# A decoder layer on one core: the retention's gates and values as seven-product pairs, another bank order in a pair's plain steps, six raw weight tiles, later first sums

## The chip, the cores and the metric

The kernel runs on one core of a Trainium2 chip. The time is device microseconds of one execution of the whole program; lower is better. All data are float32. TensorE (PE in the profile) runs the matmuls, VectorE (DVE) and ScalarE (ACT) the elementwise work, GpSimd (POOL) a few small operations and the DMAs that add while they load, SyncE (SP) issues most DMAs.

## What is computed

One layer: h = RMSNorm(x) for 256 positions of width 2048, a wide input projection of h, three token mixers on its columns (sparse attention, retention, attention into a memory), a sigmoid gate on each mixer's branch, an output projection, and a gated FFN of width 5632. The parts that the change touches are matrix products with a weight that streams in from HBM:

```
proj = h @ w_in            # columns: a_q a_k a_v i_q i_k i_w r_q r_k r_v r_g m_q gates
o_b  = silu(r_g) * groupnorm(retention(r_q, r_k, r_v))
mixed = g_a*(o_a @ w_branch_a) + g_b*(o_b @ w_branch_b) + g_c*(o_c @ w_branch_c)
x  = x + rms_norm(mixed @ w_out)
f_gate, f_up = split(rms_norm(x) @ w_ffn_in)
x  = x + rms_norm((silu(f_gate) * f_up) @ w_ffn_out)
```

r_g and r_v are 2048 columns each, so four groups of 512 columns each.

## The kernel before

**A product in three passes.** A float32 operand is split into a high and a low part. ACT casts half of a raw weight tile to `whi` (line 432), DVE subtracts to get `wlo` (line 438), and for each 128 rows of the contraction PE multiplies high by high, high by low and low by high into one PSUM bank (lines 500 to 508). A matmul has 128 by 128 of the activation as its stationary operand and 512 weight columns moving through.

**Jobs.** A job makes 512 output columns for 256 positions, in two banks of 128 positions. Its contraction of 2048 comes in four chunks of 512, and each chunk is one raw weight tile of 1 MB with two halves. So a job has 4 loads, 8 halves, 96 matmuls.

**Pairs.** Two jobs that share the activation can be made one Pair (`plan_pair`). One of the four chunks is then done with seven products of 6 matmuls in place of eight. Some of the seven use sums: `t1` (line 275, DVE) adds the first raw tile `r1` to the second, `r2`, in place, and three DMAs that add while they load (line 271, issued by POOL) change `r2` further between its uses; `make_forms` builds the sums of the activation once per chunk (DVE and ACT). A pair works in four banks, W and X for one job, Y and V for the other. Products 1, 6 and 7 go to bank X, and after each its content is taken out to an SBUF tile `snap` before more is added (`take_1`, `take_6`, `take_7`; `take_7` is the ACT operation of line 313, or a DVE operation of line 315 where a split contraction adds an earlier part). The other chunks run as plain steps: a half of a weight against both position blocks, so two banks. The string of line 394 gives the order: `152d3ddd6dd7ccc4ccc`, digits for products, `d` and `c` for plain steps of the second and the first job.

Before the change these are pairs: the gates of the first and third mixer (four pairs), the gates of the second (two), one pair of its branch product, one pair of `w_out`, eight pairs of FFN columns, and two column groups of `w_ffn_out`, as three pairs over parts of the contraction: 19 in all. The retention's four `rg` (gate) and four `rv` (value) jobs are plain jobs. After each `rv` job a generator `retain` does the retention of two heads, a step at a time between the matmuls, with DVE work and small PE and POOL steps.

**What sets the order.** There is no scheduler: `Stream.run` writes the program out unit by unit, and each engine's queue is in that order. Ahead of a unit (12 matmuls, or 6 for a product) `run` issues loads on SP as long as fewer than `RAWS` raw tiles are loaded and not yet fully split, and not more than six halves ahead (lines 467 to 471); the `whi` of three halves ahead and the `wlo` of two halves ahead; and `t1`, once `r1` and `r2` have been issued as loads and the next sum is due within six halves. One unit is also one step (`tick`) of the other work: `fast` holds the evacuations of banks, `slow` the rest (`retain`, `make_forms`, `load_x`). SP issues its DMAs in the program's order, and each waits for the tile that it fills. `turned` transposes a result through DRAM: DVE transposes, eight small DMAs on SP (line 681), one that fetches (line 685). `bcast` loads a row of gains to all partitions (line 1217, a POOL DMA); `load_x` calls it twice for each of four column groups, `fin_evac` once for each `w_ffn_out` group.

Pools: `tp` has 31 tiles of 4 KB a partition, `hp` 8 of 2 KB, `wr` (the raw tiles) `RAWS` = 5 of 8 KB, `ws` 4 each of `whi` and `wlo`.

Of the kernel before, what the change touches and what calls it, by code (L numbers as in the profile page):

```python
# [19 lines left out]
P = 128  # L20
# [130 lines left out]
class Unit:  # L151


    def __init__(self, s, muls, ready, weight=1.0, begin=None, end=None):
        self.s, self.muls, self.ready, self.weight = s, muls, ready, weight
        self.begin, self.end = begin, end


class Stream:


    RAWS = 5

# [94 lines left out]
    def plan_pair(self, pr):  # L258
# [82 lines left out]
        def plain(g, c, hf, ends):  # L341
            l = loads[g, c]
            s = self.add_item([l], 512, lambda: l.half(hf))
            pair = [acc[a] for a in ("WX", "YV")[g]]

            def stat(m):
                return lambda q: [t[c][:, 2 * hf + q, m * P:(m + 1) * P] for t in (xop.hi, xop.lo)]

            def begin():
                for a in pair:  # L350
                    self.begin(a)

            def end():
                for k in ends:
                    finish(k)
            self.add_unit(Unit(s, [(pair[m], stat(m)) for m in range(2)],
                               lambda: all((c, m) in xop.ready for m in range(2)), begin=begin,
                               end=end if ends else None))

# [81 lines left out]
    def run(self, jobs):  # L441
# [4 lines left out]
        where = {id(l): i for i, l in enumerate(loads)}  # L446
        srcs, his, los = [], [], []
        loaded, summed, added, passed = 0, 0, 0, 0.0

        def add_up():  # L450

            nonlocal summed
            if summed == len(self.sums):
                return False
            t = self.sums[summed]
            if t.after >= len(los) or any(where[id(l)] >= loaded for l in t.loads):
                return False
            t.fn()
            summed += 1
            return True  # L460

        for n, unit in enumerate(self.units):
            s = unit.s
            more = True
            while more:
                more = False
                while loaded < len(loads) and loads[loaded].first <= s + 6:
                    if sum(l.last >= len(los) for l in loads[:loaded]) >= (3 if loaded < 8 else self.RAWS):
                        break
                    self.load(loads[loaded], (4, 2, 2, 2)[loaded] if loaded < 4 else 1)  # L470
                    loaded += 1
                while added < len(self.adds) and self.adds[added].after < len(los):
# [22 lines left out]
            if summed < len(self.sums) and self.sums[summed].before <= s + 6:  # L495
                add_up()
            if unit.begin:
                unit.begin()
            self.until(unit.ready)
            hi, lo = his[s], los[s]  # L500
            for q in range(2):
                for a, parts in unit.muls:
                    xh, xl = parts(q)
                    for x, w in ((xh, hi), (xh, lo), (xl, hi)):
                        held = unit.end is not None and q == 1 and w is hi and x is xl
                        a.n += 1
                        PE.matmul(a.tile, x, w[:, q], start=a.n == 1,  # L507
                                  stop=a.n == a.total or held, skip_group_check=a.read)
            if unit.end:
# [10 lines left out]
def tile_layer(ctx: ExitStack, tc: tile.TileContext, io):  # L520
# [3 lines left out]
    const = ctx.enter_context(tc.tile_pool(name="const", bufs=1))  # L524
    tp = ctx.enter_context(tc.tile_pool(name="tp", bufs=31))
    hp = ctx.enter_context(tc.tile_pool(name="hp", bufs=8))
# [284 lines left out]

    def pair(rows=in_T):

        two = jobs.pop()
        jobs.append(Pair(jobs.pop(), two, rows))
# [372 lines left out]
    def values(i):  # L1188
        def evac(ps):
            tmp = []  # L1190
            yield from copied(tmp, "rv", "x")(ps)
            st.slow.append(retain(i, tmp[0]))
            if i == 3:
                st.slow.append(make_forms(ob, 0))
        return evac

    for i in range(4):
        proj("rg", i, swish(i))
        proj("rv", i, values(i))

    def after_merge(i):
# [13 lines left out]
    def bcast(src, i, n="gain"):  # L1215
        t = H([P, 512], n)
        G.dma_start(t, bass.AP(tensor=src.tensor, offset=src.offset + 512 * i, ap=[[0, P], [1, 512]]))
        return t
# [177 lines left out]
    def ffn_up(j):  # L1396
        def evac(ps):
            if j == NF - 1:
                st.slow += [make_forms(act, c) for c in (0, 4, 8)]
            t = ffn.pop(j)  # L1400
            for m in range(2):
                V.scalar_tensor_tensor(t[m], ps[m], rmt["ffn", m], t[m], op0=ALU.mult, op1=ALU.mult)
                yield "free" if m else None
            yield
            turned(t, split_turned(act))
        return evac

    for j in range(NF):
        jobs.append(Job(h2, io["w_ffn_in"][2 * j], KD, 512, ffn_gate(j), lead="" if j else "first"))
        jobs.append(Job(h2, io["w_ffn_in"][2 * j + 1], KD, 512, ffn_up(j)))  # L1410
        if j in BLOCKS:
            pair(lambda g: (in_T if g else in_H)(g))

# [9 lines left out]
    def fin_evac(i):  # L1423
        def evac(ps):
            gt = bcast(io["g_post_ffn"], i)
            if i == 1:
                for k in kept:
                    xr.append(T([P, 2, 512], n="xr"))
                    nc.sync.dma_start(xr[-1], k)
                yo3["g"] = bcast(io["g_post_ffn"], 3)  # L1430
            yo3[i] = T([P, 2, 512], n="yo3")
            yield
# [110 lines left out]
```

## Time and profile before

| what | value |
| --- | --- |
| time, median of 3 runs | 1880.06 us (1879.97 to 1880.45) |
| the profiled execution's own time | 1882.16 us |
| span of its records | 1880.4 us |
| PE busy | 1861.9 us, 99% |
| DVE busy | 1241.9 us, 66% |
| ACT busy | 938.7 us, 50% |
| POOL busy | 75.7 us, 4% |
| mean granted clock of TensorE | 0.998 |
| DMA | 432.59 MB, mean 230 GB/s |

Busy time of PE counts modelled ends of pipelined matmuls, so a matmul reads as 0.39 us although the next one starts about 0.23 us after it. The distance from start to start is what a matmul costs in a stream. The chain is the profile's own walk back from the last instruction; where it lies on PE over hundreds of matmuls, its time divided by their number is that distance.

### The profile page before, as it was taken

What the parts mean: (1) busy time and instruction counts of PE and PEld (TensorE: products, weight loads), DVE (VectorE), ACT (ScalarE), POOL (GpSimd) and SP (SyncE); (2) the same over time, 40 slices, a digit from 0 to 9 for tenths busy, and PEclk for the clock granted to TensorE, in tenths of its full rate; (3) what the DMA queues carried; (4) which work ended last, traced back from release to release, by engine and by line L of the source; (5) the groups of instructions that cost most, each with busy time, mean ns of one, the idle gap of its engine ahead of it and who ended that gap; (6) DMA issues with size and microseconds to landing.
All of it is one profiled execution on the core that took longest, in us unless ns stands there. A gap on an engine that the chain in (4) does not pass through costs nothing.

```text
span 1880.4 us, 21857 instructions
## 1 busy us (share of the span) xinstructions
PE 1861.9 (99%) x8330; PEld 1533.2 (82%) x8330; DVE 1241.9 (66%) x1509; ACT 938.7 (50%) x1111; POOL 75.7 (4%) x98
## 2 busy tenths in 40 slices
PE   9999999999999999999999999999999999999998
PEld 6888878888888888888887887888888888887886
DVE  5766767777656654556777676756767676666664
ACT  7744444545545444444555444545555555445442
POOL 0000000000000000000100000000000000000000
PEclk9999999999999999999999999999999999999999
DMA  9847565547676756555668684578888887577782
GB/s 372 307 164 265 209 241 188 183 177 247 216 243 217 226 207 221 192 196 189 211 218 296 213 280 157 208 233 286 275 272 257 258 248 244 186 262 226 238 291 84
DMA packets 106201, 432.59 MB, mean 230 GB/s; under 512 B 12000, under 2 KB 43232, under 8 KB 64624
## 3 DMA queue, kind: packets, MB, share of 16 engines
q1 hardware_dynamic: 96720, 398.12, 57.3%
q0 software_dynamic: 9232, 33.07, 10.1%
q8 instruction: 65, 1.06, 0.2%
q14 instruction: 40, 0.33, 0.0%
q10 hardware_dynamic: 144, 0.01, 0.0%
HBM read 411.22 MB, written 19.92 MB: 229 GB/s over the span
## 4 chain that ended last, share of the span: by engine, by line
PE 92%; DVE 3%; DMA 2%; issue 2%; ACT 1%; SPq 0%; POOL 0%; POOLq 0%; DVEq 0%; ACTq 0%
PE acc L507 89%; DVE wlo L438 1%; DMA raw<-in_w_mem_kv 1%; DMA gain<-in_g_pre_ffn 0%; DMA gain<-in_g_post_ffn 0%; PE bk L1049 0%; DMA raw<-in_w_in 0%; PE bk L1031 0%; PE bk L923 0%; ACT whi L432 0%; DMA raw<-in_w_out 0%; PE bk L996 0%; DVE y L673 0%; PE bk L1163 0%; PE bk L1016 0%
## 5 line engine op out<-in xcount | busy, mean ns | idle before, releaser
L432 ACT CAST whi<-raw 128x1024 fp32r<-128x1024 f32 (+1 forms) x731 | 759.9, 1043 | 798.1 <-PE acc L507 715.8
L438 DVE TENSOR_TENSOR wlo<-raw,whi 128x1024 fp32r<-128x1024 f32 (+1 forms) x731 | 875.0, 1208 | 329.4 <-ACT whi L432 326.2
L507 PE MATMUL acc<-whi,hi 128*128 128x512 f32 (+2 forms) x2498 | 978.1, 392 | 3.2 <-ACT snap L313 1.9
L507 PE MATMUL acc<-wlo,hi 128*128 128x512 f32 (+2 forms) x2498 | 969.6, 388 | 3.2 <-DVE wlo L438 3.1
L507 PE MATMUL acc<-whi,lo 128*128 128x512 f32 (+2 forms) x2498 | 968.9, 388 | 0.0
L507 PEld LDWEIGHTS acc<-whi,hi 128*128 128x128 f32 x2498 | 469.9, 188 | 106.6 <-ACT snap L313 9.3
L507 PEld LDWEIGHTS acc<-wlo,hi 128*128 128x128 f32 x2498 | 470.0, 188 | 99.3 <-DVE wlo L438 6.5
L507 PEld LDWEIGHTS acc<-whi,lo 128*128 128x128 f32 x2498 | 469.7, 188 | 95.3
L507 PE MATMUL acc<-wlo,fhi 128*128 128x512 f32 x152 | 59.3, 390 | 1.0 <-DVE wlo L438 1.0
L507 PE MATMUL acc<-whi,flo 128*128 128x512 f32 x152 | 59.4, 391 | 0.6 <-DVE flo L743 0.6
L507 PE MATMUL acc<-whi,fhi 128*128 128x512 f32 x152 | 59.7, 393 | 0.0
L384 DVE TENSOR_TENSOR snap<-acc,snap 128x512 f32<-128x512 f32 x38 | 26.2, 689 | 34.0 <-PE acc L507 26.4
L363 DVE TENSOR_TENSOR snap<-acc,snap 128x512 f32<-128x512 f32 x19 | 13.1, 692 | 44.5 <-PE acc L507 44.5
L271 POOL DMA_DIRECT2D raw<-in_w_in x18 | 15.5, 860 | 630.1 <-DMA raw<-in_w_in 423.4
L712 DVE TENSOR_TENSOR lo<-turned,hi 128x1024 fp32r<-128x1024 f32 x16 | 19.6, 1227 | 31.4 <-ACT hi L711 31.3
L507 PEld LDWEIGHTS acc<-wlo,fhi 128*128 128x128 f32 x152 | 28.6, 188 | 7.2 <-DVE wlo L438 1.4
L271 POOL DMA_DIRECT2D raw<-in_w_ffn_in x24 | 20.5, 852 | 342.8 <-DVE wlo L438 268.5
L507 PEld LDWEIGHTS acc<-whi,flo 128*128 128x128 f32 x152 | 28.5, 188 | 6.9 <-DVE flo L743 1.0
L507 PEld LDWEIGHTS acc<-whi,fhi 128*128 128x128 f32 x152 | 28.6, 188 | 5.8
L308 DVE TENSOR_TENSOR snap<-snap,acc 128x512 f32<-128x512 f32 x19 | 13.0, 687 | 30.2 <-PE acc L507 30.2
L275 DVE TENSOR_TENSOR raw<-raw,raw 128x1024 f32<-128x1024 f32 x19 | 23.2, 1221 | 14.7 <-DMA raw<-in_w_in 11.6
L798 DVE TENSOR_TENSOR rp<-acc,cos 128x512 f32<-128x512 f32 (+2 forms) x24 | 14.5, 604 | 20.8 <-PE acc L507 20.8
(197 smaller groups left out, 701.6 us busy)
## 6 DMA issues: line engine op xcount, KB each, us to landing
raw<-in_w_in SPq DMA_DIRECT2D x132, 1024.0 KB, 6.8
raw<-in_w_ffn_in SPq DMA_DIRECT2D x88, 1024.0 KB, 5.6
raw<-in_w_ffn_out SPq DMA_DIRECT2D x44, 1024.0 KB, 6.5
raw<-in_w_branch_b SPq DMA_DIRECT2D x16, 1024.0 KB, 5.3
raw<-in_w_out SPq DMA_DIRECT2D x16, 1024.0 KB, 5.5
d<-y SPq DMA_DIRECT2D x240, 64.0 KB, 1.8
turned<-d SPq DMA_DIRECT2D x30, 512.0 KB, 6.2
raw<-in_w_mem_kv SPq DMA_DIRECT2D x12, 1024.0 KB, 11.9
```

The source lines that it names most:

```text
L271: return lambda: G.dma_start(l.half(hf).rearrange("p a b -> p (a b)"), pr.jobs[g].w[cs][:, 1024 * k:1024 * k + 1024], accum_op=ALU.add)
L275: V.tensor_add(r2.half(0), r2.half(0), r1.half(0))
L308: V.tensor_sub(row(1, 0), row(1, 0), acc["X"].tile)
L363: V.tensor_add(t, acc["W"].tile, t)
L384: V.tensor_add(row(1, m), acc[a].tile, row(1, m))
L432: self.nc.scalar.copy(hi[:, sl], src[:, sl])
L438: self.nc.vector.tensor_sub(lo[:, sl], src[:, sl], hi[:, sl].bitcast(F32))
L507: PE.matmul(a.tile, x, w[:, q], start=a.n == 1, stop=a.n == a.total or held, skip_group_check=a.read)
L712: V.tensor_sub(l4, v, h4.bitcast(F32))
L798: V.tensor_tensor(t1, s4, cos, op=ALU.mult)
```

## The change

1. `rg` i and `rv` i become a Pair for each of the four i: four more pairs.
2. The plain steps of every pair are ordered by bank: all six matmuls of a half into one bank, then the six into the other. Before, they went three by three.
3. `RAWS` is 6, and loads may be issued up to eight halves ahead, not six. `tp` shrinks from 31 to 29 tiles to make room.
4. `t1` is written into the program, as long as it isn't urgent, only when both its loads were issued at least four units ago.
5. `bcast` issues on SP, not on POOL.
6. `make_forms(ob, 0)` is queued after the retention of i = 1, not of i = 3. `make_forms(act, 8)` is queued 24 units after the start of the third `w_ffn_out` group's evacuation (`fin_evac(2)`), not with the other two.
7. The first row of a pair's `snap` comes from `hp`, as one tile (`in_TH`); before, most pairs took it from `tp`.

```diff
-    RAWS = 5
+    RAWS = 6
...
             self.add_unit(Unit(s, [(pair[m], stat(m)) for m in range(2)],
                                lambda: all((c, m) in xop.ready for m in range(2)), begin=begin,
-                               end=end if ends else None))
+                               end=end if ends else None, by_bank=True))
...
-        def add_up():
+        def add_up(age=0):
...
-            if t.after >= len(los) or any(where[id(l)] >= loaded for l in t.loads):
+            if t.after >= len(los) or any(where[id(l)] >= loaded or since[where[id(l)]] > n - age for l in t.loads):
...
-                while loaded < len(loads) and loads[loaded].first <= s + 6:
+                while loaded < len(loads) and loads[loaded].first <= s + 8:
...
             if summed < len(self.sums) and self.sums[summed].before <= s + 6:
-                add_up()
+                add_up(4)
...
-            for q in range(2):
-                for a, parts in unit.muls:
-                    xh, xl = parts(q)
...
+            order = [(a, parts, q) for q in range(2) for a, parts in unit.muls]
+            if unit.by_bank:
+                order.sort(key=lambda o: unit.muls.index(o[:2]))
+            for a, parts, q in order:
+                xh, xl = parts(q)
...
-    tp = ctx.enter_context(tc.tile_pool(name="tp", bufs=31))
+    tp = ctx.enter_context(tc.tile_pool(name="tp", bufs=29))
...
+    def in_TH(g):
+        return in_T(g) if g else [H([P, 512], "snap")]
+
+    def pair(rows=in_TH):
...
-            if i == 3:
+            if i == 1:
                 st.slow.append(make_forms(ob, 0))
...
         proj("rv", i, values(i))
+        pair()
...
-        G.dma_start(t, bass.AP(tensor=src.tensor, offset=src.offset + 512 * i, ap=[[0, P], [1, 512]]))
+        nc.sync.dma_start(t, bass.AP(tensor=src.tensor, offset=src.offset + 512 * i, ap=[[0, P], [1, 512]]))
...
-                st.slow += [make_forms(act, c) for c in (0, 4, 8)]
+                st.slow += [make_forms(act, c) for c in (0, 4)]
...
+            if i == 2:
+                st.call(24, lambda: st.slow.append(make_forms(act, 8)))
```

In all the program has 24 matmuls fewer with a `whi` or `wlo` as the moving operand, 7926 against 7950.

**The order on PE** after product 7 of the first FFN pair, before. `acc_1851` is bank X, `acc_1860` bank W; the first three rows are the end of product 7:

```order
L507 MATMUL acc_1851_9717<-whi_1877_9847,fhi_1800_9426 128x512
L507 MATMUL acc_1851_9717<-wlo_1880_9860,fhi_1800_9426 128x512
L507 MATMUL acc_1851_9717<-whi_1877_9847,flo_1801_9427 128x512
L507 MATMUL acc_1860_9746<-whi_1879_9858,hi_1714_9008 128x512
L507 MATMUL acc_1860_9746<-wlo_1883_9878,hi_1714_9008 128x512
L507 MATMUL acc_1860_9746<-whi_1879_9858,lo_1715_9009 128x512
L507 MATMUL acc_1851_9717<-whi_1879_9858,hi_1714_9008 128x512
```

And the same place in the changed kernel, with `acc_1883` as X and `acc_1892` as W:

```order
L510 MATMUL acc_1883_9793<-whi_1908_9922,flo_1834_9505 128x512
L510 MATMUL acc_1892_9823<-whi_1911_9935,hi_1747_9086 128x512
L510 MATMUL acc_1892_9823<-wlo_1915_9955,hi_1747_9086 128x512
L510 MATMUL acc_1892_9823<-whi_1911_9935,lo_1748_9087 128x512
L510 MATMUL acc_1892_9823<-whi_1911_9935,hi_1747_9086 128x512
L510 MATMUL acc_1892_9823<-wlo_1915_9955,hi_1747_9086 128x512
L510 MATMUL acc_1892_9823<-whi_1911_9935,lo_1748_9087 128x512
L510 MATMUL acc_1883_9793<-whi_1911_9935,hi_1747_9086 128x512
```

Between product 7 and the next matmul into X there were three matmuls, and now there are six.

**The order on SP** in the second pair of the second mixer's gates, before: the eight sends of a `turned` (d_1486), and the raw loads around them:

```order
L427 DMA raw_1482_7773<-in_w_in 128x2048
L681 DMA d_1486_7795<-y_1485_7792 32x4x128 x8
L427 DMA raw_1492_7826<-in_w_in 128x2048
L427 DMA raw_1499_7876<-in_w_in 128x2048
L685 DMA turned_1502_7889<-d_1486_7795 128x1024
```

The same in the changed kernel, with d_1519 as the sends; raw_1515 holds the same weights as raw_1492 above:

```order
L427 DMA raw_1509_7819<-in_w_in 128x2048
L688 DMA turned_1512_7831<-d_1491_7733 128x1024
L427 DMA raw_1515_7851<-in_w_in 128x2048
L684 DMA d_1519_7873<-y_1518_7870 32x4x128 x8
L427 DMA raw_1527_7915<-in_w_in 128x2048
```

The load that stood just behind the eight sends now stands ahead of them.

**The order on POOL and SP** around the `w_out` pair. On POOL before, the adding loads of the pair (raw_1558) and the gains stood in one queue:

```order
L1217 DMA gain_1565_8240<-in_g_pre_ffn 128x512
L271 DMA raw_1558_8215<-in_w_out 128x1024
L1217 DMA gain_1579_8330<-in_g_post_mix 128x512
L1217 DMA gain_1580_8332<-in_g_pre_ffn 128x512
L271 DMA raw_1558_8215<-in_w_out 128x1024 x2
```

On SP now, the gains stand behind a raw load and an `xr` load:

```order
L427 DMA raw_1606_8367<-in_w_out 128x2048
L1235 DMA xr_1611_8406<-in_x 128x2x512
L1224 DMA gain_1612_8408<-in_g_post_mix 128x512
L1224 DMA gain_1613_8410<-in_g_pre_ffn 128x512
L427 DMA raw_1618_8426<-in_w_out 128x2048
```

POOL's queue now holds only the adding loads there, three in a row.

## Rows read from the trace of the kernel before

**Rows 1.** The page's first part: busy time, share, instructions of each engine.
```profile
PE 1861.9 (99%) x8330; PEld 1533.2 (82%) x8330; DVE 1241.9 (66%) x1509; ACT 938.7 (50%) x1111; POOL 75.7 (4%) x98
```

**Rows 2.** PE's waits over the whole run: total us, times, longest us.
```profile
PE acc L507 <- DVE wlo L438: 4.1, 8, 1.0
...
PE bk L1005 <- DVE lg L983: 0.5, 1, 0.5
PE bk L1290 <- DVE yl L1284: 0.5, 1, 0.5
```

**Rows 3.** The chain that ended last, in the FFN: start us, us, what.
```profile
1177.80 98.64 PE acc L507 x435
...
1276.45 42.46 PE acc L507 x186
```

**Rows 4.** Timeline after product 7 of the first FFN pair: start, us, engine.
```profile
1275.80 0.60 ACT L313 ACTIVATE snap<-acc 128x512 f32<-128x512 f32 x1 [0.30 <-PE acc L507]
...
1276.05 0.39 PE L507 MATMUL acc<-whi,lo 128*128 128x512 f32 x1
...
1276.45 0.50 PE L507 MATMUL acc<-whi,hi 128*128 128x512 f32 x1
```

**Rows 5.** The page's groups of DVE: count, busy us, mean ns, idle before.
```profile
L438 DVE TENSOR_TENSOR wlo<-raw,whi 128x1024 fp32r<-128x1024 f32 (+1 forms) x731 | 875.0, 1208 | 329.4 <-ACT whi L432 326.2
...
L363 DVE TENSOR_TENSOR snap<-acc,snap 128x512 f32<-128x512 f32 x19 | 13.1, 692 | 44.5 <-PE acc L507 44.5
...
L275 DVE TENSOR_TENSOR raw<-raw,raw 128x1024 f32<-128x1024 f32 x19 | 23.2, 1221 | 14.7 <-DMA raw<-in_w_in 11.6
```

**Rows 6.** PE's timeline: the starts of matmuls after an idle time, in brackets.
```profile
884.03 0.50 PE L507 MATMUL acc<-wlo,hi 128*128 128x512 f32 x1 [0.59 <-DVE wlo L438]
...
939.36 0.50 PE L507 MATMUL acc<-whi,flo 128*128 128x512 f32 x1 [0.56 <-DVE flo L743]
...
1007.42 0.50 PE L507 MATMUL acc<-whi,hi 128*128 128x512 f32 x1 [1.95 <-ACT snap L313]
...
1080.07 0.50 PE L507 MATMUL acc<-wlo,hi 128*128 128x512 f32 x1 [0.90 <-DVE wlo L438]
...
1702.38 0.51 PE L507 MATMUL acc<-wlo,fhi 128*128 128x512 f32 x1 [0.98 <-DVE wlo L438]
```

**Rows 7.** The chain behind the stall at 1007 us: start us, us, what.
```profile
1007.42 35.24 PE acc L507 x147
```

**Rows 8.** That stretch's window: us, busy PE, PEld, DVE, ACT, POOL, PEclk, DMA share, GB/s.
```profile
1008.30:1011.60 3.30, 3.30 (x10) 2.53 (x9) 3.19 (x3) 2.17 (x4) 0.00 (x0) 0.50 1.02 432
```

**Rows 9.** Timeline of ACT ahead of the stall at 1007 us.
```profile
1005.82 1.04 ACT L432 CAST whi<-raw 128x1024 fp32r<-128x1024 f32 x1 [4.02 <-DVE wlo L438]
1006.77 0.59 ACT L313 ACTIVATE snap<-acc 128x512 f32<-128x512 f32 x1
```

**Rows 10.** Timeline of SP's issues in the same stretch.
```profile
993.13 5.56 SPq L681 DMA_DIRECT2D d<-y  x8
998.79 2.30 SPq L427 DMA_DIRECT2D raw<-in_w_in  x2
```

**Rows 11.** The page's DMA issues: count, KB each, median us to landing.
```profile
raw<-in_w_in SPq DMA_DIRECT2D x132, 1024.0 KB, 6.8
```

**Rows 12.** The chain behind the stalls at 884 and 1080 us.
```profile
874.62 6.91 DMA raw<-in_w_in
...
1069.79 8.37 DMA gain<-in_g_pre_ffn
```

**Rows 13.** Timeline of DVE just before the stalls at 1080 and 1702 us.
```profile
1078.18 0.69 DVE L1234 TENSOR_TENSOR xg<-xr,gain 128x512 f32<-128x512 f32 x1 [2.14 <-DMA gain<-in_g_pre_ffn]
...
1700.50 0.69 DVE L1421 TENSOR_TENSOR yo<-acc,gain 128x512 f32<-128x512 f32 x1 [3.77 <-DMA gain<-in_g_post_ffn]
```

**Rows 14.** SP's waits over the whole run: total us, times, longest us.
```profile
SPq L427 <- DVE wlo L438: 1039.5, 226, 11.9
```

**Rows 15.** Windows, columns as in rows 8: retention; pair with retention; FFN pairs.
```profile
811.00:854.00 43.00, 43.00 (x193) 35.72 (x193) 25.81 (x38) 19.26 (x20) 3.13 (x2) 1.00 0.54 203
889.00:932.00 43.00, 42.99 (x196) 35.46 (x195) 33.56 (x50) 24.16 (x28) 4.80 (x4) 1.00 0.69 212
1251.00:1591.00 340.00, 339.93 (x1491) 279.10 (x1490) 237.20 (x232) 187.60 (x200) 19.53 (x23) 1.00 0.83 261
```

More of the change, by code (lines that the diff above doesn't have):

```diff
@@ L151, with __init__ @@
 class Unit:
-    def __init__(self, s, muls, ready, weight=1.0, begin=None, end=None):
-        self.s, self.muls, self.ready, self.weight = s, muls, ready, weight
+    def __init__(self, s, muls, ready, weight=1.0, begin=None, end=None, by_bank=False):
+        self.s, self.muls, self.ready, self.weight, self.by_bank = s, muls, ready, weight, by_bank
         self.begin, self.end = begin, end
 class Stream:
-    RAWS = 5
+    RAWS = 6
     def __init__(self, nc, wr, ws, acc, nm, T):
@@ L446, in run @@
         where = {id(l): i for i, l in enumerate(loads)}
-        srcs, his, los = [], [], []
+        srcs, his, los, since = [], [], [], []
         loaded, summed, added, passed = 0, 0, 0, 0.0
-        def add_up():
+        def add_up(age=0):
             nonlocal summed
@@ L470, in run @@
                     self.load(loads[loaded], (4, 2, 2, 2)[loaded] if loaded < 4 else 1)
+                    since.append(n)
                     loaded += 1
@@ L500, in run @@
             hi, lo = his[s], los[s]
-            for q in range(2):
-                for a, parts in unit.muls:
-                    xh, xl = parts(q)
[L504 to L508, printed above, removed]
+            order = [(a, parts, q) for q in range(2) for a, parts in unit.muls]
[3 more added lines that the diff above has]
+                xh, xl = parts(q)
+                for x, w in ((xh, hi), (xh, lo), (xl, hi)):
+                    held = unit.end is not None and q == 1 and w is hi and x is xl
+                    a.n += 1
+                    PE.matmul(a.tile, x, w[:, q], start=a.n == 1,
+                              stop=a.n == a.total or held, skip_group_check=a.read)
             if unit.end:
@@ L810, in in_H @@
         return [H([P, 512], "snap") for _ in range(2)]
-    def pair(rows=in_T):
+    def in_TH(g):
+        return in_T(g) if g else [H([P, 512], "snap")]
+    def pair(rows=in_TH):
         two = jobs.pop()
@@ L1411, in tile_layer @@
         if j in BLOCKS:
-            pair(lambda g: (in_T if g else in_H)(g))
+            pair()
     ssq3 = const.tile([P, 2, 4], F32, name="ssq3")
```

## The prediction

> **What bounds the kernel.** I read the page's first part, then the list of PE's waits, the chain of work that ended last, PE's timeline around its idle times, and last the windows of the stages that change. PE is busy for 99 % of the span and no other engine for more than 66 % [rows 1], so the end is set by how many matmuls PE runs and how closely they follow one another. Its waits are few: the longest list entries sum to under 10 us [rows 2]. In a stretch without any wait 435 matmuls take 98.64 us [rows 3], so one costs 0.2268 us from start to start; the 0.39 us that the timeline gives one is a modelled length. Whatever the change does to DVE, ACT or the DMAs counts only where it opens or closes a gap between matmuls. The sum is made against the profiled execution, whose own 1882.16 us is 2.10 above the median of the runs; its span of 1880.4 lies 0.34 above that median, so differences in the span are carried to the median as they are.
>
> **A. Fewer matmuls.** A new pair does one chunk with seven products of six matmuls where eight stood, so each of the four saves six: 24 x 0.2268 = 5.44 us. All of it is on the path, since the retention's window has PE busy for 43.00 of 43 us [rows 15]. The Trainium skill, "TensorE: Matmul & The Clock Gate", section "Wait — 56ns, not 53.3ns?", gives 215.7 ns for a matmul of 512 columns that follows another at full clock, which would make this term 5.18 us. The trace differs by 5 %, and its 0.2268 us stands.
>
> **B. Bank order.** An FFN pair has 186 matmuls and takes 42.46 us [rows 3]; 186 x 0.2268 is 42.18, so 0.28 us per pair is lost. The place: after product 7, ACT takes bank X out from 1275.80 for 0.60 us, and the next matmul into X starts at 1276.45, 0.40 us after the matmul before it at 1276.05 [rows 4]. Only three matmuls of bank W (0.68 us) cover that copy. In the new order six do, 1.36 us: enough for the 0.60 us copy with the 0.30 us it waits for product 7's end [rows 4], and for a DVE operation on a bank, 0.69 us by the nearest rows, `take` excepted [rows 5]. The same matmuls run either way, so nothing is given up. There are 19 such pairs, one first sum each [rows 5]; the nineteenth stalls longer and is C. 18 x 0.28 = 5.0 us; with the decimals of the quotient (98.64 / 435 x 186 = 42.177) it is 18 x 0.283 = 5.09. The other end is the visible gap alone, 0.40 - 0.227 = 0.17, or 3.1 us. I take the chain's, since its piece holds the whole pair, the slower steps around the gap too. The new pairs never pay it.
>
> **C. The stall at 1007 us.** PE idles 1.95 us there [rows 6]; to the start before it that is 2.34 us, 2.11 above a step. For 1008.3 to 1011.6 the granted clock is 0.50, the 1.2 GHz level [rows 8], and 147 matmuls take 35.24 us instead of 33.33: 1.91 more [rows 7]. Together 4.02 us. Behind it: ACT had idled 4.02 us until `whi` at 1005.82, and the snapshot that PE waits for stood behind that cast [rows 9]. The cast's raw load went out at 998.79 only, after eight sends that held SP for 5.56 us from 993.13 [rows 10], and a load lands 6.8 us after its issue [rows 11]. In the changed order this load stands ahead of the eight sends, which gives it 5.56 us or more, more than ACT's 4.02 of waiting. So the stall goes, and with it the low clock, which came only behind that idle time. Late next there would be the sends themselves; what fetches them stands behind at least one more load.
>
> **D. Four other stalls.** Each costs its idle time plus 0.39 - 0.227 of the modelled length, plus 0.11 for the step behind it. At 884.03: 0.86 us. A raw load issued at 874.62 [rows 12] comes late to `t1`, and `wlo` queues behind `t1` on DVE; the sixth raw tile issues it sooner. At 939.36: 0.83, since `flo` of the sums for `ob` was written three matmuls ahead of its use; it now stands 391 ahead. At 1080.07: 1.17. `xg` on DVE waited for a gain load [rows 13] that took 8.37 us behind POOL's adding loads [rows 12]; gains now go by SP. At 1702.38: 1.25, a gain again, for which DVE idled 3.77 us [rows 13]. All four starts stand in [rows 6]; the sum is 4.11 us.
>
> **E. What I cost at nothing.** Each new pair adds on DVE three `wlo` (3 x 1.21), one `t1` (1.22) and four snapshot operations of 0.69 [rows 5], 7.6 us; on ACT three casts of 1.04 and up to three copies of 0.60 [rows 9], 4.9 us. In the retention's window DVE is busy 25.81 of 43 us and ACT 19.26 [rows 15]; with these it is 33.4 and 24.2 of about 42.2. Their cover is PE's stream. The nearest row is the pair that already runs beside the retention's rest, 33.56 of DVE with PE at 42.99 [rows 15], so I take zero. The other end is a stall like that of C, 4.02 us, for a pair with a burst of DVE work just ahead of a `wlo`. POOL issues three adding loads per pair at about 19.53 / 23 = 0.85 us each [rows 15], beside an idle queue. DMA: a window of 43 us at 203 GB/s moves 8.7 MB; three half loads add 1.6 MB, about 244 GB/s, and the FFN pairs hold PE at 339.93 of 340 with 261 [rows 15]. The two tiles fewer of `tp` have no row; by the nearest they cost between nothing and one stall like 1702's, 1.25 us. The order shows no tile with a waiter close behind its last user, so nothing. The later `t1` and `make_forms(act, 8)`, 45 matmuls or 10 us ahead of its use where DVE's two operations and ACT's need under 4, cost nothing as long as DVE's queue is not more than 6 us deep. The gains on SP stand behind raw loads, which waited 226 times for 1039.5 us in all, 4.6 on average and 11.9 at most [rows 14]. By the order the last gain of the `w_out` pair stands 48 matmuls, 10.9 us, ahead of the DVE operation that uses it. It needs at most the 6.8 us of a raw load [rows 11], so 4.1 us of waiting are free and a wait of 11.9 would cost up to 7.8. I take zero, and give the other end to the fourth rival.
>
> **Sum.** 5.44 + 5.09 + 4.02 + 4.11 = 18.66 us: 1880.06 - 18.66 = **1861.4 us** (the span 1861.7).
>
> **Rivals.**
> 1. *The new pairs stall a little.* `retain` steps, `t1` and the snapshots meet in DVE's queue and `wlo` comes late. For: DVE's mean idle share hides bursts, and `wlo` is already PE's commonest releaser [rows 2]. Against: the pair at 889 us does not stall between its 884 and 939. Three pairs with 0.83 as at 939.36 and one with 4.02 as at 1007 give back 6.5: 1867.9. Chance 0.17.
> 2. *Slower: DVE becomes the bound of the four pairs.* If the added 7.6 us of DVE per pair all came onto the path, because `retain` is a chain that waits for PE and POOL steps and holds DVE's queue, and the clock fell once in each pair as at 1007 (1.91), the price is 4 x 9.5 = 38 us: 1899.4. It decides from 18.66 / 4 = 4.7 us a pair, more than the worst stall of the whole profile gives. Against: 33.4 of 42.2. Chance 0.04, and 0.03 for a half-way case near 1878, 16.1 us from four stalls like C's.
> 3. *The loads are not earlier after all.* SP's raw loads wait for `wlo` to give a tile back [rows 14]; if the sixth tile is used up as fast, the loads still go out after the sends in time, and C and 884 stay: 4.02 + 0.86 back, 1866.3. Chance 0.08.
> 4. *The gains come as late by SP.* On SP they follow 1 MB loads, and one load takes 6.8 us to land [rows 11]; if a gain waits for those ahead of it, 1080 and 1702 stay: 2.42 back, 1863.8. For: the 4.1 us of slack is less than SP's mean wait of 4.6. Against: only two or three gains stand so close, and the sixth raw tile shortens those waits. Chance 0.11. The Trainium skill, "DMA: Bandwidth & Descriptors", "Queues, rings and completion order", says that an engine's ring is worked off in order while rings of other queues take turns, which would speak for this rival; no row of before shows a gain on SP.
>
> **Range and chances.** The forecast has 0.57. Below it there are the other small waits: `wlo` 4.1 - (0.59 + 0.90 + 0.98) = 1.6, and the two of 0.5 [rows 2], if the moved order ends them too: 1858.8. Above, the range goes to the first rival, which takes in the third and fourth: 1868.0. Left out are the second with its half-way case and mixtures. 0.2 % is 3.8 us, about what a measurement can tell from no change. Faster by more: all but the second, 0.93; within: the half-way case, 0.03; slower: 0.04.
>
> **What would show it.** Right: 8306 matmuls on PE; FFN pairs of 42.2 us for 186; four new pairs with as much; no stretch at 0.50 clock near the second mixer's pairs; no gain or raw load as releaser of DVE before a PE gap; the wait on a snapshot gone from PE's list. Wrong in A's cover: PE gaps on `wlo` within the four new pairs, with DVE near full there. Wrong in C: ACT still idle before a `whi` in that pair, with SP's sends just ahead of its load. Wrong in B: the pieces stay at 42.46. Wrong as a whole: a sum of PE's waits above 10 us, or PE's distance per matmul other than 0.2268.

## The result, and the profile after

The changed kernel takes 1865.38 us (median of 4 runs, 1864.94 to 1865.60) against 1880.01 (1879.33 to 1880.45): ratio 0.9922, 95 % interval 0.9905 to 0.9939. That is 14.6 us faster; the forecast was 1861.4, in a range of 1858.8 to 1868.0, so the change gave 4.0 us less than forecast. The profiled execution took 1865.49 us, with a span of 1863.7.

The page's first part, with the columns of [rows 1], and the list of PE's waits, as in [rows 2]:

```profile
PE 1849.2 (99%) x8306; PEld 1528.1 (82%) x8306; DVE 1269.6 (68%) x1541; ACT 955.7 (51%) x1135; POOL 79.4 (4%) x98
```

```profile
PE acc L510 <- DVE wlo L438: 2.1, 6, 0.8
PE acc L510 <- ACT whi L432: 1.5, 2, 1.0
...
PE bk L1011 <- DVE lg L989: 0.5, 1, 0.5
PE bk L1297 <- DVE yl L1291: 0.5, 1, 0.5
```

PE runs the 24 matmuls fewer. The wait on a snapshot and the one on `flo` have left its list. The chain of waits, with the columns of [rows 3], has one piece where before it was cut at every FFN pair:

```profile
462.50 292.41 PE acc L510 x1290
...
1165.74 684.14 PE acc L510 x3018
```

3018 matmuls run without one gap from 1165.74 us to 1849.88 us, 5 us before the last matmul starts, at 684.14 / 3018 = 0.2267 us each, against 0.2268 in [rows 3]. No FFN pair is interrupted any more.

The two traces differ by 16.9 us at the last matmul. To see where these come from, the program is cut at the first matmul of each stage, in both timelines, and the stage lengths are compared (us; the last column has the prediction's terms for the stage):

| stage, from its first matmul to the next stage's | before | after | difference | predicted |
| --- | --- | --- | --- | --- |
| start to the first pair | 439.53 | 440.21 | +0.67 | 0 |
| four pairs of the first and third mixer, with plain jobs between | 262.74 | 261.50 | -1.24 | -1.13 (B) |
| the four gate and value stages of the retention | 187.11 | 182.33 | -4.77 | -6.30 (A, 884) |
| second mixer's gates, first pair | 47.45 | 47.23 | -0.21 | -0.28 (B) |
| its branch product, pair | 43.33 | 42.16 | -1.17 | -1.11 (B, 939) |
| second mixer's gates, second pair | 46.01 | 42.16 | -3.85 | -4.02 (C) |
| `w_out` pair | 44.61 | 43.11 | -1.50 | -1.45 (B, 1080) |
| eight FFN pairs | 339.73 | 337.28 | -2.46 | -2.26 (B) |
| first part of the split `w_ffn_out` pairs | 43.78 | 42.16 | -1.62 | -1.53 (B, 1702) |
| the other two parts | 74.24 | 73.44 | -0.80 | -0.57 (B) |

All other stages are equal within 0.02 us. The sum at the last matmul is -16.93, predicted -18.66. The four stages of the retention are -1.36, -1.35, -0.11 and -1.95 one by one: 6 x 0.2267 = 1.36 in the first two, and a loss in the third and fourth. In the third, PE stands still twice (its timeline, idle time and releaser in brackets):

```profile
827.57 0.50 PE L510 MATMUL acc<-wlo,hi 128*128 128x512 f32 x1 [0.33 <-DVE wlo L438]
...
829.50 0.50 PE L510 MATMUL acc<-wlo,hi 128*128 128x512 f32 x1 [0.27 <-DVE wlo L438]
```

DVE's timeline ahead of them:

```profile
822.84 1.22 DVE L438 TENSOR_TENSOR wlo<-raw,whi 128x1024 fp32r<-128x1024 f32 x1
823.97 1.30 DVE L676 STREAM_TRANSPOSE y<-yo 128x512 f32<-128x512 f32 x2
825.19 1.18 DVE L734 TENSOR_TENSOR whole<-hi,lo 128x1024 f32<-128x1024 f32 x1
826.30 1.22 DVE L438 TENSOR_TENSOR wlo<-raw,whi 128x1024 fp32r<-128x1024 f32 x1
827.43 0.42 DVE L737 TENSOR_TENSOR whole<-whole 128x256 f32<-128x256 f32 x1
```

L734 and L737 belong to `make_forms(ob, 0)`, which the change moved to this place. Two transposes and the first of these sums, 2.3 us together, stand between two `wlo`, and PE uses up a half in 12 x 0.227 = 2.7 us. It is what the prediction named as a sign of being wrong in A's cover, gaps on `wlo` in a new pair with DVE near full. The window around it (columns as in [rows 8]) has DVE at 14.54 of 15 us:

```profile
815.00:830.00 15.00, 14.41 (x62) 11.28 (x62) 14.54 (x27) 7.96 (x9) 1.54 (x1) 1.00 0.22 64
```

At the place of C the order did what it says. SP's and ACT's timelines of after:

```profile
978.90 0.44 SPq L427 DMA_DIRECT2D raw<-in_w_in  x1
985.13 8.13 SPq L684 DMA_DIRECT2D d<-y  x8
993.91 0.35 SPq L427 DMA_DIRECT2D raw<-in_w_in  x1
...
995.25 0.33 SPq L688 DMA_DIRECT2D turned<-d  x1
```

```profile
996.80 1.06 ACT L432 CAST whi<-raw 128x1024 fp32r<-128x1024 f32 x1 [1.71 <-PE acc L510]
998.11 0.60 ACT L313 ACTIVATE snap<-acc 128x512 f32<-128x512 f32 x1 [0.26 <-PE acc L510]
```

The load at 978.90 is the one that stood behind the sends before. The eight sends now hold SP for 8.13 us, more than the 5.56 of [rows 10], and PE doesn't pay for it: ACT waits for PE alone, where in [rows 9] it had waited 4.02 us and PE's snapshot stood behind that cast.

### The profile page after: what moved, and what is told of

The parts are those of the page before. It is cut to its first block, busy times and chain, and to the rows that moved or that the text cites. A ratio compares the mean times of both kernels' runs of the same rounds, so it can differ in the third digit from the quotient of the medians.

```text
span 1863.7 us, 21935 instructions
## 1 busy us (share of the span) xinstructions
PE 1849.2 (99%) x8306; PEld 1528.1 (82%) x8306; DVE 1269.6 (68%) x1541; ACT 955.7 (51%) x1135; POOL 79.4 (4%) x98
## 4 chain that ended last, share of the span: by engine, by line
PE 96%; DVE 2%; DMA 1%; issue 1%; ACT 0%; POOL 0%; SPq 0%; POOLq 0%; DVEq 0%
PE acc L510 93%; DVE wlo L438 1%; DMA raw<-in_w_mem_kv 1%; PE bk L1037 0%; PE bk L1055 0%; PE bk L929 0%; PE bk L1002 0%; DVE y L676 0%; PE bk L1169 0%; PE bk L1022 0%; PE bk L1168 0%; PE bk L1155 0%; PE bk L1167 0%; PE bk L1011 0%; PE bk L661 0%
## 5 line engine op out<-in xcount | busy, mean ns | idle before, releaser
L432 ACT CAST whi<-raw 128x1024 fp32r<-128x1024 f32 (+1 forms) x743 | 772.0, 1043 | 763.6 <-PE acc L510 701.9
L438 DVE TENSOR_TENSOR wlo<-raw,whi 128x1024 fp32r<-128x1024 f32 (+1 forms) x743 | 889.7, 1208 | 317.3 <-ACT whi L432 311.8
L510 PE MATMUL acc<-whi,hi 128*128 128x512 f32 (+1 forms) x2458 | 958.3, 390 | 1.5 <-ACT whi L432 1.5
L510 PE MATMUL acc<-wlo,hi 128*128 128x512 f32 (+1 forms) x2458 | 952.1, 387 | 2.3 <-DVE wlo L438 2.1
L510 PE MATMUL acc<-whi,lo 128*128 128x512 f32 (+1 forms) x2458 | 951.6, 387 | 0.0
L510 PE MATMUL acc<-whi,fhi 128*128 128x512 f32 x184 | 72.7, 395 | 0.0
L510 PE MATMUL acc<-wlo,fhi 128*128 128x512 f32 x184 | 71.7, 390 | 0.0
L510 PE MATMUL acc<-whi,flo 128*128 128x512 f32 x184 | 71.7, 389 | 0.0
L271 POOL DMA_DIRECT2D raw<-in_w_in x30 | 25.8, 860 | 791.7 <-DVE wlo L438 398.2
L1106 DVE TENSOR_TENSOR gate<-gate,acc 128x512 f32<-128x512 f32 x21 | 14.4, 684 | 23.4 <-PE acc L510 23.4
```

The source lines that it names most:

```text
L271: return lambda: G.dma_start(l.half(hf).rearrange("p a b -> p (a b)"), pr.jobs[g].w[cs][:, 1024 * k:1024 * k + 1024], accum_op=ALU.add)
L432: self.nc.scalar.copy(hi[:, sl], src[:, sl])
L438: self.nc.vector.tensor_sub(lo[:, sl], src[:, sl], hi[:, sl].bitcast(F32))
L510: PE.matmul(a.tile, x, w[:, q], start=a.n == 1, stop=a.n == a.total or held, skip_group_check=a.read)
L1106: V.tensor_tensor(g[:, m], g[:, m], ps[m], op=ALU.mult)
```

## The experiments

All medians below stand against runs of the kernel before on the same chip, whose median was 1880.0 in the first two groups (experiments 1 to 3 and 11; 4, 5, 8 and 9) and 1880.7 in the third (6, 7, 10 and 12). So medians of different groups can be compared to within about 0.7 us. Stage lengths come from one profiled execution of each kernel.

**1. The kernel before, again** (no edit).

> The kernel before, unchanged, several executions with their clocks. The profiled execution of before took 1882.16 us and its timed runs 1880.06. Theory: the 1.91 us at the 1.2 GHz level behind the stall at 1007 us fell into that execution only, so the runs at about 1880.0 have a mean clock of 0.999 and a span near 1878.3, and a profile with an own time near 1880.0 shows PE at full clock behind 1007 us; the stall then costs 2.1 us, not 4.0. Rival: every execution has the low clock (0.998 in each), and the 2.1 us lie somewhere else.

Measured: 1880.24 us, 12 executions from 1878.16 to 1883.65. Its profiled execution took 1882.75 us, and it has the stall and the low clock again. Over these 12 and the 17 beside them, 18 with a mean clock of 0.999 have a median of 1880.06, 10 with 0.998 one of 1882.07. But the two groups overlap (1877.87 to 1881.68, and 1878.15 to 1883.65). So the low clock explains a part of the spread, and how much of C's 4.0 us a median execution pays stays open: both profiles of before are of slower ones. Another part is D's. In this second profile the first split `w_ffn_out` pair takes 42.63 us where the first has 43.78; the stall at 1702 us is not there. A third part is the start of the program: the first pair begins at 439.53 us in the first profile and at 441.39 in the second. **The profiled execution of before took 2.1 us more than the median.** That this lies in waits of C and D is likely, since its start is not late, but no profile of a median execution shows it.

**2. Bank order alone** (with the ordering code of change 2 in `run`).

```diff
...
-                               end=end if ends else None))
+                               end=end if ends else None, by_bank=True))
```

> Before, with the plain steps of pairs by bank and nothing else. Theory: 18 waits on a snapshot go, 0.31 us each by the two traces, 5.6 us, and the wait at 1007 us shrinks by the 0.68 us of three more matmuls in front of it: 1873.7 to 1874.4. Rival (only the visible gap of 0.17 us is given back, and the later steps are paid anyway): 3.1 us, 1876.9.

Measured: 1873.75 us (ratio 0.9961, 0.9949 to 0.9973), 6.3 us faster; the theory holds, the 3.1 us of the visible gap do not. Each FFN pair takes 42.16 us from its first matmul to the next pair's, against 42.47. In the profile the second gates pair has no gap either (42.16 us, before 46.01):

```profile
984.81 27.20 PE acc L509 x120
```

That is the whole of its chain from 985 to 1012 us, with five raw tiles and the load still behind the sends. I had not expected this. The cast of that load starts 5.7 us after its issue here (997.70 to 1003.43 on the timelines), 7.0 in [rows 9, 10], and six matmuls cover 0.68 us more than three; the executions spread from 1871.96 to 1874.26, and the profiled one is the fastest.

**3. The four pairs alone** (`in_TH` as in change 7).

```diff
+        pair(in_TH)
```

> Before, with the four gate and value jobs as pairs and nothing else (five raw tiles, old bank order). Theory: 24 matmuls of 0.2268 us less, 5.44, and four new waits of 0.31 us on a snapshot, 1.2: 1875.8, with every other stall of before in place. Rival: the retention's DVE work beside a pair needs the sixth raw tile and the earlier loads, and stalls in two or more of the four pairs eat up the gain: 1878 to 1882.

Measured: 1898.33 us (ratio 1.0095, 1.0082 to 1.0108): **18 us slower**, beyond both theories. Three of the four stages are 52 to 55 us long, where after has 46 to 47. The chain of waits behind the first:

```profile
778.23 1.22 DVE y L673 x2
...
782.75 0.02 SPq L427
782.77 0.04 issue
782.81 5.48 DMA raw<-in_w_in
...
789.56 1.23 DVE wlo L438
790.79 0.04 issue
790.83 1.20 PE acc L507 x4
```

and DVE's and PE's timelines there:

```profile
788.41 1.23 DVE L275 TENSOR_TENSOR raw<-raw,raw 128x1024 f32<-128x1024 f32 x1 [6.73 <-DMA raw<-in_w_in]
```

```profile
790.83 0.50 PE L507 MATMUL acc<-wlo,hi 128*128 128x512 f32 x1 [3.75 <-DVE wlo L438]
...
792.48 0.63 PE L507 MATMUL acc<-wlo,hi 128*128 128x512 f32 x1
```

Two transposes of the retention release eight sends on SP; the pair's raw load stands behind the sends; `t1` (L275) stands in DVE's queue and waits 6.73 us for that load, with `wlo` behind it. It is the stall of 884 us, three times over. SP's and DVE's timelines of the kernel before have the same three things there, with a wait of 6.92 us:

```profile
870.18 3.84 SPq L681 DMA_DIRECT2D d<-y  x8
874.13 0.88 SPq L427 DMA_DIRECT2D raw<-in_w_in  x2
```

```profile
881.61 1.23 DVE L275 TENSOR_TENSOR raw<-raw,raw 128x1024 f32<-128x1024 f32 x1 [6.92 <-DMA raw<-in_w_in]
```

In the pairs-only kernel PE idles 3.75, 4.98 and 3.49 us in the three places, against 0.59 at 884 us, and each time the clock falls after it (seven to twelve matmuls of 0.427 us). It isn't DVE's work: a window over the second of these stalls has DVE at 16.76 of 25 us (columns as in [rows 8]).

```profile
820.00:845.00 25.00, 20.01 (x87) 15.96 (x86) 16.76 (x27) 10.15 (x11) 1.78 (x2) 0.97 0.49 176
```

Not all of the 18 us lies there. The branch product's pair takes 46.80 us instead of 43.33, since PE waits 2.2 us there for `fhi` of the sums of `ob` (experiment 12 has the same), and the first split `w_ffn_out` pair takes 46.29 instead of 43.78.

Two parts of the change could be the cure of the three stalls: the sixth raw tile with the longer look ahead, or the later `t1`. Three runs tell them apart.

**4. Five raw tiles.**

```diff
-    RAWS = 6
+    RAWS = 5
...
-                while loaded < len(loads) and loads[loaded].first <= s + 8:
+                while loaded < len(loads) and loads[loaded].first <= s + 6:
```

> The changed kernel with five raw tiles and loads at most six halves ahead, as before. The four pairs alone made the kernel 18.3 us slower: three of them stand still for about 6 us, because two transposes on DVE release eight sends on SP, a raw load stands behind these, and the first sum t1 waits on DVE for that load with the wlo behind it. Theory one, the sixth tile cures this by putting the load ahead of the sends: without it the three stalls come back, 1876 to 1884. Theory two, the later place of t1 cures it, since t1 then no longer holds DVE's queue while the load is under way: 1865 to 1868.

**5. First sums as early as before.**

```diff
-                add_up(4)
+                add_up()
```

> The changed kernel with the first sums placed as before, as soon as both loads are issued. Theory one (the sixth raw tile is the cure, the place of t1 is not needed): within 0.5 us of the changed kernel, 1865 to 1866. Theory two (the place of t1 is the cure): DVE waits at t1 for a load of 5 to 7 us in each of the three pairs that run beside a retention, 1870 to 1884.

**6. Neither** (the edits of 4 and 5 together).

> The changed kernel with five raw tiles, loads at most six halves ahead, and the first sums as soon as both loads are issued. So far each of the two cures alone kept the new pairs free of stalls. Theory: they stand in for one another, and without both the three stalls of the pairs-only kernel come back, 6.0, 8.3 and 5.7 us by its trace against the changed one (20 us), on top of the 8.0 us that five tiles cost with the sums late: 1888 to 1894. Rival: the pairs-only stalls came from the old bank order or from POOL's gains, and this kernel is at 1873 to 1876, as with five tiles alone.

Measured: 1873.38 with five tiles, 1865.02 with early sums, 1886.60 with both (ratio to before 1.0030, 1.0019 to 1.0042). Each cure alone keeps the new pairs free: with five tiles they take the same 42.16, 46.22, 47.5 and 46.5 us as after, with early sums 42.16, 46.22, 47.85 and 46.54, and without both 42.16, 52.11, 56.53 and 52.20. In the pairs, then, theory two holds for the first run and theory one for the second: neither cure is needed as long as the other is there. The third run shows that they stand in for one another: 20.7 us are lost in the four stages. Its time is 1.4 us below the forecast, and the first run lies between its two theories because of losses outside the pairs. DVE's waits at `t1`, with early sums and with neither (after has none):

```profile
DVE raw L275 <- DMA raw<-in_w_in: 5.0, 2, 2.7
```

```profile
DVE raw L275 <- DMA raw<-in_w_in: 23.9, 4, 6.8
```

The 8.0 us that the first run loses against after lie elsewhere, by the trace: 4.87 in the second gates pair (C), 1.64 in the first pair of all, 1.36 and 0.74 in a split pair and the `w_out` pair. C's chain is back in full there, the bank order notwithstanding:

```profile
995.52 6.76 DMA raw<-in_w_in
...
1003.33 0.60 ACT snap L313
1003.93 0.04 issue
1003.97 8.24 PE acc L510 x28
```

The third run has five tiles too, and none of these losses is in its profile: 42.16 us in the second gates pair, 43.11 in the `w_out` pair. Its median, 21.2 us above after, has room for little more than the 20.7 in the four stages. So these losses come with five tiles and late sums together, and not with five tiles alone. What in the late sums brings them isn't shown.

**7. Six raw tiles on the kernel before** (with the two tiles fewer in `tp` and what they need).

```diff
-    RAWS = 5
+    RAWS = 6
...
-                while loaded < len(loads) and loads[loaded].first <= s + 6:
+                while loaded < len(loads) and loads[loaded].first <= s + 8:
```

> Before, with six raw tiles and loads up to eight halves ahead, 29 tiles in tp with what that needs (first snapshots from hp, the sums of the last ffn chunk later), and nothing else. Theory (the load ahead of the sends is the cure of C and of 884): C's 2 to 4 us and 0.86 go, 1875.2 to 1877.2. Rival: the stall at 1007 us goes only with the bank order: 1879.2.

Measured: 1877.57 us (ratio 0.9982, 0.9973 to 0.9991), so 3.1 us faster. In the traces the second gates pair falls from 46.01 to 42.46 with the old bank order, and the retention's last stage from 48.45 to 47.57, which is 884's 0.86. The theory holds at both places; the median lies 0.4 us above its range. The two traces differ by 3.55 and 0.88 us there, 4.4 in all, and the medians by 3.1. One reason is that the profiled execution of this run is the fastest of its eleven, 1.1 us below the median. Another is a loss that was not expected: the second split pair takes 43.41 us instead of 42.56, since PE waits 0.93 us there for the snapshot of line 315, which stands behind a sum of `make_forms(act, 8)` on DVE. Experiment 9 has the same wait.

**8. Gains on POOL.**

```diff
-        nc.sync.dma_start(t, bass.AP(tensor=src.tensor, offset=src.offset + 512 * i, ap=[[0, P], [1, 512]]))
+        G.dma_start(t, bass.AP(tensor=src.tensor, offset=src.offset + 512 * i, ap=[[0, P], [1, 512]]))
```

> The changed kernel with the gains' loads issued by POOL again. Theory (term D): the stall near 1080 us (1.17) comes back and the one near 1702 us (1.25 in one of two profiles of before, none in the other) in some executions: 1866.5 to 1867.8. Rival: with the adding loads three in a row and the sixth tile the gains on POOL are early enough, 1865.4.

Measured: 1866.81 us, 1.4 more than after and in the theory's range, from 1864.79 to 1868.71. In its profile both stalls are back, near 1068 us with 0.46 us in place of 1.17, and near 1688 us with 3.77 in place of 1.25:

```profile
DVE yo L1428 <- DMA gain<-in_g_post_ffn: 4.6, 1, 4.6
DVE xg L1241 <- DMA gain<-in_g_pre_ffn: 1.4, 1, 1.4
```

```profile
1688.48 0.50 PE L510 MATMUL acc<-wlo,fhi 128*128 128x512 f32 x1 [1.88 <-DVE wlo L438]
```

The rest of the 3.77 is seven matmuls at the 1.2 GHz level behind it. The fastest of the five executions is as fast as after: gains on POOL are a cost that comes and goes.

**9. Plain steps three by three.**

```diff
-                               end=end if ends else None, by_bank=True))
+                               end=end if ends else None))
```

> The changed kernel with the plain steps of a pair three by three again. Theory: 23 waits on a snapshot, 19 old and 4 new pairs, of 0.31 us (0.40 in the two with an earlier part): 7.3 us, 1872.7, and nothing else, since the load behind the stall at 1007 us is early now. Rival: the bank order was also what removed the stall at 1007 us, as the bank order alone already did with five raw tiles; then 2 to 4 us more, 1874.7 to 1876.7.

Measured: 1873.44 us, 8.06 more. Its FFN pairs stand in the chain as before:

```profile
1266.23 42.46 PE acc L510 x186
```

By stages 0.31 us is lost in nearly every pair, and 1.27 in the second split one. That one shows a cost of moving `make_forms(act, 8)` which six matmuls cover and three don't. DVE's timeline has its sum (L734) and a `wlo` just ahead of the snapshot of line 315, and PE waits 0.93 us for that snapshot:

```profile
1749.70 1.22 DVE L734 TENSOR_TENSOR whole<-hi,lo 128x1024 f32<-128x1024 f32 x1
1750.84 1.22 DVE L438 TENSOR_TENSOR wlo<-raw,whi 128x1024 fp32r<-128x1024 f32 x1
1751.97 0.68 DVE L315 TENSOR_TENSOR snap<-snap,acc 128x512 f32<-128x512 f32 x1
```

The second gates pair takes 42.49, so it is the sixth tile that ends C there, and the theory is nearer (7.3) than the rival (9.3 to 11.3).

**10. Gate and value jobs plain.**

```diff
-        pair()
```

> The changed kernel with the retention's gate and value jobs as plain jobs. Theory (term A, with what the new pairs lose): 24 matmuls more, 5.44 us, less the 1.5 us that the third and fourth new pair stand still, if the sums of ob find a quieter DVE: 1869.3 to 1870.8. Rival (the stall at 884 us comes back in a plain job with six tiles too): 1871.7.

Measured: 1869.55 us, in the theory's range: 4.2 more than after and 5.8 more than the best version below, with its own runs of before 0.7 higher. By stages, 43.52 and 47.57 us here stand against 42.16 and 46.22 in the first two new pairs of after, 1.35 to 1.36 each. So a new pair is worth its 1.36 us, and the four their 5.44, where nothing stalls. The last stage takes 47.57 without the stall of 884 us, so the rival doesn't hold.

**11 and 12. The place of the sums of `ob`**: after the retention of i = 2, and of i = 3.

```diff
-            if i == 1:
+            if i == 2:
```

In the second of these runs the new line is `if i == 3:`.

> The changed kernel with the sums of ob queued after the retention of i = 2 instead of i = 1. In the changed kernel the third new pair stands still twice, at 827.6 and 829.5 us, while DVE does these sums and a transpose between two wlo. Theory: these 1.25 us come from the sums' place and go: 1864.1, and no new stall near 875 us. Rival: the burst goes with the sums into the fourth pair: 1865.4.

> The changed kernel with the sums of ob queued after the retention of i = 3, as before. Theory (term D, 939 us): the 1.25 us of the third new pair go and a wait of 0.83 us for flo comes back in the second pair of the second mixer's gates: 1864.6 to 1865.1, above the 1863.74 of the version with i = 2. Rival: no wait comes back, 1863.7.

Measured: **1863.74 us with i = 2** (ratio to before 0.9909, 0.9897 to 0.9922), the best version of the study; its third stage takes 46.29 us instead of 47.46, with no gap. With i = 3 it is 1868.49, above both its theory and its rival: the third stage is free too, but the branch product's pair (where the stall at 939 us of before lies) takes 46.50 instead of 42.16. PE now waits there 2.2 us, with the low clock behind it, for `fhi` and not for `flo`, since that cast stands on ACT behind a snapshot and a gate:

```profile
932.33 0.59 ACT L296 COPY snap<-acc 128x512 f32<-128x512 f32 x1 [0.26 <-PE acc L510]
932.82 0.72 ACT L1097 ACTIVATE gate<-snap,rstd 128x512 f32<-128x512 f32 x1
933.44 1.03 ACT L744 CAST fhi<-whole 128x1024 fp32r<-128x1024 f32 x1
```

So the move of the sums took 4.3 us from this stage in the changed kernel and not 0.83, and it went one retention too far. Against i = 2, by the stages of the traces, i = 1 pays 1.2 us and i = 3 pays 4.3; by the medians it is 1.6 and 4.8, of which up to 0.7 can be the group's.

## Why the prediction was right, and where it was not

**A** held: -1.36 and -1.35 us in the two undisturbed stages, and 0.2267 us per matmul, against 0.2268. The Trainium skill, "TensorE: Matmul & The Clock Gate", section "Wait — 56ns, not 53.3ns?", has 0.2157; the trace of after disagrees, with 0.2267 over 3018 matmuls without a gap.

**B** held, and was a little low: 0.31 us a pair (42.47 to 42.16), 0.40 in the split pairs, against 0.283. The choice of the chain's piece over the visible gap was right; the lower end of 3.1 us is refuted by experiments 2 and 9. Over all pairs B gave about 5.7 us (the table's rows less D's terms) instead of 5.09.

**C** held in the trace (-3.85 against -4.02, of which experiment 7 gives 3.55 to the sixth tile and the earlier loads and leaves 0.30 to the bank order). Its cause, the load behind the sends, is shown by experiment 7, and none of the eight profiles with six tiles has this stall. Not foreseen: the bank order can hide it too. With bank order and five tiles the stall is absent in experiments 2 and 6, where the load goes out 18.0 us after the stage's first matmul, and full in experiment 4, where it goes out after 20.5. So C was not the sixth tile's alone, and the two terms overlap.

**D** held in place. 884 went, 939 went, and the gains went; their loads by SP land after 4.8, 6.3 and 9.0 us (least, median, most), by POOL in the kernel before they land after 6.2, 8.2 and 11.3. The fourth rival is wrong at these places: in the profile of after no operation of DVE waits for a gain. By the rule of the Trainium skill, "DMA: Bandwidth & Descriptors", section "Queues, rings and completion order", that each DMA engine consumes the descriptors of a ring in order, the gains could have come late behind the 1 MB loads; here they did not come late enough to be waited for. Mis-sized: 1702 (1.25 in one profile of before, absent in the other) and 939 (4.3 in the changed kernel).

**The step that failed first** is the sentence that differences of the span are carried to the median as they are. It set a span (1880.4) beside a median of whole times (1880.06) and found them 0.34 apart. But the whole time is longer than the span by 1.7 to 2.1 us in every run on record, so like for like the profiled execution was 2.1 us above its median. Taken from its own time the same sum gives 1882.16 - 18.66 = 1863.5. The terms C and D were read from waits, and other executions have at least some of them smaller or not at all (1702 in experiment 1). The traces differ by 16.7 us in the span, the medians by 14.6: half of the 4.0 us that the forecast was too low.

**The second** is in E: `make_forms(ob, 0)` at its new place was costed at nothing, because it stood 391 matmuls ahead of its use. What counts was what it is put beside. It cost PE 1.25 us in the third stage, of which 1.17 go in experiment 11. Another 0.25 is lost in the fourth, where a matmul starts at 846.08 us as its `wlo` ends at 846.02; that one stays wherever the sums are put (46.53 and 46.49 us in experiments 11 and 12, 46.49 in after). The first rival was of this kind, priced at 6.5 us, and it set the upper end of the range. The 2.1 us of the first step stood in no rival. Another 0.7 us are in the start of the program, where the first matmuls came later; over all 14 profiles the first pair starts between 438.61 and 441.39 us, and in the two of before at 439.53 and 441.39, so this is the execution's and not the change's. Against these losses B gave 0.6 us more than forecast.

**Right for a reason not given** was E's zero for the new pairs. I took DVE's idle share as their cover. DVE was busy for 64 % of the second retention stage in the pairs-only kernel, which is 18 us slower, and for 73 % in after: what had to be covered was a wait in DVE's queue, `t1` for a load behind the sends. Two parts of the change prevent it in the new pairs, each by itself. The slower rival, DVE at its limit, was the wrong mechanism; the right one stood in the profile as the stall at 884 us, which I had explained in D and not carried over to three pairs that run under the same retention.

**The third rival** (loads no earlier) is refuted by SP's timeline of after and by experiment 7.

## What to carry to other kernels

A stall that a profile shows once is a price list for every new place of the same make: before adding four blocks, look for the one block that already stalls, and ask whether the new ones have the same neighbours. An instruction that waits for a transfer should enter an in-order queue late, or its transfer be issued early; either was enough for the new pairs here, and the second also ended the stalls at 884 and 1007 us. Terms read from one profile are only as good as that execution, so waits on DMAs are best checked in a second profile before they are summed.

## What the runs showed of the hardware that was not expected

A wait of 2 us on PE can cost twice that, and not only at the place of C. After a stall in the kernel with neither cure the window shows 11 matmuls in 4 us, at 0.50 of the clock, which is the 1.2 GHz level:

```profile
846.00:850.00 4.00, 4.00 (x11) 3.14 (x10) 3.81 (x4) 0.16 (x1) 0.00 (x0) 0.50 0.72 248
```

Idle times of 1.88, 1.95, 2.97, 3.49 and 3.75 us were each followed by seven or eight matmuls of about 0.427 us, one of 4.98 us by twelve, one of 2.23 us (experiment 12) by three, one of 1.32 us (experiment 3) and the four of 0.56 to 0.98 us [rows 6] by none. The executions of a kernel seem to draw together when its waits on DMAs go: they spread over 4.3 us in 5 with five tiles and over 3.9 in 5 with the gains on POOL, but over 0.7 in 4 of after. With so few executions this is not shown; four of before lay within 1.1 us (1879.33 to 1880.45), and 29 within 5.8 (1877.87 to 1883.65).
